# A decoder trunk's last norm in parts: squares a product earlier, scalings in place, and a ring of ten for raw activations

## The chip, the core and the metric

The kernel runs on one core of one Trainium2 chip. The core has five engines with an instruction queue each: TensorE (PE, the matmuls), VectorE (DVE), ScalarE (ACT), GpSimd (POOL) and SyncE (SP, which here only issues transfers). Each queue is worked off in order. The metric is the time of one execution on the device, in microseconds (us), the median over some runs. A profile is one further execution, taken by the hardware profiler.

## The reference

One layer of a decoder in fp32, for 2048 tokens of width 1024, then a last norm. What matters here is the end:

```python
def rmsnorm(x, w):
    xf = x.astype(jnp.float32)
    xf = xf * lax.rsqrt(jnp.mean(xf * xf, axis=-1, keepdims=True) + NORM_EPS)
    return (xf * w.astype(jnp.float32)).astype(x.dtype)

def conv_ffn(h, w_up, conv_w, conv_b, w_down):
    gv = h @ w_up
    g = causal_dwconv(gv[..., :D_FF], conv_w, conv_b)
    v = gv[..., D_FF:]
    return (jax.nn.silu(g) * v) @ w_down
...
        h = rmsnorm(x, ffn_norm_w[i])
        x = x + conv_ffn(h, ffn_w_up[i], ffn_conv_w[i], ffn_conv_b[i], ffn_w_down[i])
    return rmsnorm(x, final_norm_w)
```

D_FF is 2816. The change touches the product with w_down and the last norm.

## The kernel before

**Products in halves.** Every fp32 operand is split in two parts that TensorE takes: `halves` (L95) has ScalarE copy the hi part (L98) and VectorE subtract it for the lo part (L99). `mm3` (L120) adds three matmuls for each block of 128 rows of the contraction: hi by hi (L123), hi by lo (L124), lo by hi (L125), each 128x512. `load` (L109) issues a transfer on SP's queue (L111). `rstd` (L127) makes the root of a norm: a VectorE instruction (L130), then a power on GpSimd (L131).

**Stages.** `trunk` runs its stages one after the other, the last two being `stage_up` (gate and value of the feed-forward block) and `stage_down` (the product with w_down, the residual and the last norm). Both use schemes of seven products of sums of blocks. `stage_up` does them for each of two token blocks and 22 column blocks, in the order 1, 6, 5, 3, 7, 4, 2 (`products`, L1008), with 12 matmuls for each product, so a last group of 84 matmuls stands ahead of `stage_down`. Product number n reads its activations from a pool `Hn` of 8 tiles, and raw weights come into `R` (8 tiles).

**stage_down** has seven products (m = 0 to 6, the table `prods`), each for eight pairs of token tiles (p), that is 56 steps of 33 matmuls (`steps`, L1481). `right(m)` makes the 11 weight blocks of a product: raw tiles of w_down through a ring `R` of four, with a sum of two of them on VectorE (L1447) in the products from m=2 on, then halves into the W rings. The eleven of the next product are made one or two per step of the present one. `left(m, p)` makes the activations of one step, one step ahead: three chunks (4, 4 and 3 blocks, 512, 512 and 384 columns); for each it loads one or two raw tiles into the ring `A` (two, except in m=2 and m=3), adds them in place on VectorE (L1462), and makes halves into the rings C and B of six tiles, three hi and three lo in turn for each step. The result of a step lies in PSUM (a ring of eight) and is added to one or two halves of the 1024-wide accumulators of the tiles, kept in `X` (tiles 0 to 7) and `Y` (8 to 15): the first time by a ScalarE copy (L1504), later by VectorE (L1506). In m=2 and m=3 the residual x2 of a tile is loaded into the ring `O` and added (L1494 to L1497).

**The last norm.** A tile of odd number is complete after its step of m=5, one of even number after its step of m=6. `finish(t)` (L1471) then does all of it: ScalarE squares the tile's 1024 columns into a tile of `O` with the sum beside it (L1474), the root (L130, L131), two scalings of 512 columns into `O` (L1478) and two transfers out (L1479).

**Pools and order.** The names of the pools of a stage are laid out in SBUF in the order of its `k.pools` line, and the next stage's pools use the same memory; a tile that overlaps one of the stage before waits for the last reader of that very tile. `stage_up` has this line:

```python
    wa, ev, up, h1, gp, wb, cp, *hs, rp, sp = k.pools(cx, "u", ("V", 4), ("E", 8), ("U", 4), H(1), ("G", 4, 576), ("W", 14), ("C", 1, 1024), H(3), H(7), H(4), H(2), H(6), H(5),
                                                      ("R", 8), ("S", 2))
```

A pair ("V", 4) is four tiles of 512 columns, a third number another width; H(n) is ("Hn", 8). The order of instructions on each engine is set by the framework's scheduler; it can differ from the order of the code.

Of the kernel before, what the change touches and what calls it, by code (L numbers as in the profile page):

```python
# [9 lines left out]
F32 = mybir.dt.float32  # L10
F32R = mybir.dt.float32r
I32 = mybir.dt.int32
AF = mybir.ActivationFunctionType
ALU = mybir.AluOpType
AX = mybir.AxisListType
P = 128
# [1071 lines left out]
def ring(n, pools):  # L1088

    it = cycle([p for p in pools for _ in range(n)])  # L1090
    return lambda *args: next(it)(*args)
# [327 lines left out]
def stage_down(k, cx, a, d, out, T, NK=11):  # L1419


    nc, tc, V, S, G = k.nc, k.tc, k.V, k.S, k.G
    NT = T // 128

    W = lambda i: (f"W{i}", 8)
    xa, w0, xb, rp, ar, sp, cb, fp, *ws, wr, ca = k.pools(cx, "d", ("X", NT // 2, 1024), W(0), ("Y", NT // 2, 1024), ("O", 2, 1152), ("A", 6), ("S", 2), ("C", 6), ("F", 1, 1024),
                                                          W(3), W(4), W(1), W(2), ("R", 4), ("B", 6))
    wp, ac = ring(8, [w0] + ws[2:] + ws[:2]), ring(6, [ca, cb])

    prods = [(((1, 0), (1, 1), 1), ((0, 0),), ((1, 0, 1), (1, 1, -1))),  # L1430
# [6 lines left out]
    chunks = ((0, 4), (4, 8), (8, 11))  # L1437
    op = lambda s: ALU.add if s > 0 else ALU.subtract

    def right(m):  # L1440
        r = prods[m][1]
        for j in range(NK):
            raws = [k.load(a["w_down"][kh * NK + j][:, dh * 512:dh * 512 + 512], wr()) for kh, dh in r[:2]]
            x = raws[0]
            if len(r) > 1:
                x = sp()
                V.tensor_tensor(x, raws[0], raws[1], op=op(r[2]))  # L1447
            hi, lo = wp(F32R), wp(F32R)
            k.halves(x, hi, lo)
            yield hi, lo  # L1450

    def left(m, p):
        l, got = prods[m][0], []
        for lo_, hi_ in chunks:
            n = (hi_ - lo_) * 128
            raws = []
            for t, kh in l[:2]:
                raw = ar()[:, 0:n]
                k.load(d["act"][2 * p + t][:, kh * NK + lo_:kh * NK + hi_, :], raw.rearrange("p (a n) -> p a n", n=128))
                raws.append(raw)  # L1460
            if len(l) > 1:
                V.tensor_tensor(raws[0], raws[0], raws[1], op=op(l[2]))  # L1462
            h, lw = ac(F32R)[:, 0:n], ac(F32R)[:, 0:n]
            k.halves(raws[0], h, lw)
            got += [(h[:, j * 128:j * 128 + 128], lw[:, j * 128:j * 128 + 128]) for j in range(hi_ - lo_)]
        return got
    acc, here = {}, set()
    fw = fp()
    G.dma_start(out=fw, in_=a["final_norm_w"].partition_broadcast(P))

    def finish(t):  # L1471
        x, xs = acc[t], rp()[:, 0:1024]
        ss = k.sm.tile([P, 1], F32, tag="ss", name="ss")
        S.activation(xs, x, AF.Square, accum_out=ss)  # L1474
        k.rstd(ss, ss, 1.0 / 1024, 1e-6)
        for nh in range(2):
            s = slice(nh * 512, nh * 512 + 512)
            V.scalar_tensor_tensor(xs[:, s], x[:, s], ss[:, 0:1], fw[:, s], op0=ALU.mult, op1=ALU.mult)  # L1478
            nc.sync.dma_start(out=out[t * 128:t * 128 + 128, s], in_=xs[:, s])  # L1479
    NP = NT // 2  # L1480
    steps = [(m, p) for m in range(7) for p in range(NP)]  # L1481
    gen = right(0)
    Lh = {steps[0]: left(*steps[0])}
    W = list(gen)
    for n, (m, p) in enumerate(steps):
        if p == 0:
            Wn, gen = [], right(m + 1) if m < 6 else None
        for t, dh, _ in prods[m][2]:
            t += 2 * p
            if t not in acc:  # L1490
                acc[t] = xa() if t < NT // 2 else xb()
        if n + 1 < len(steps):
            Lh[steps[n + 1]] = left(*steps[n + 1])
        if m in (2, 3):  # L1494
            x, xt = rp()[:, 0:1024], (m - 2) * NP + p
            nc.sync.dma_start(out=x, in_=d["x2"][xt * 128:xt * 128 + 128, :])
            V.tensor_tensor(acc[xt], acc[xt], x, op=ALU.add)  # L1497
        ps = k.ps()
        k.mm3(ps, [(*l, *w) for l, w in zip(Lh.pop((m, p)), W)])
        for t, dh, sign in prods[m][2]:  # L1500
            o = acc[2 * p + t][:, dh * 512:dh * 512 + 512]
            if (2 * p + t, dh) not in here:
                here.add((2 * p + t, dh))
                S.activation(o, ps, AF.Copy, scale=float(sign))  # L1504
            else:
                V.tensor_tensor(o, o, ps, op=op(sign))  # L1506
        if gen:
            for _ in range(2 if p else 1):
                w = next(gen, None)
                if w:  # L1510
                    Wn.append(w)
            if p == NP - 1:
                Wn += list(gen)
        if p == NP - 1:
            W = Wn
        if m >= 5:
            finish(2 * p + (1 if m == 5 else 0))


def trunk(tc, a, out, T):  # L1520
    with ExitStack() as cx:
# [28 lines left out]
        with ExitStack() as c1:  # L1550
            stage_down(k, c1, a, d, out, T)
# [40 lines left out]
```

## Time and profile before

| | us |
|---|---|
| median of three runs | 2668.95 (2668.3 to 2670.01) |
| profiled execution, its own time | 2667.42 |
| its span, first to last instruction | 2665.7 |
| PE busy in the span | 2603.0 |
| DVE, ACT, POOL busy | 2121.5, 1358.0, 407.3 |

The profiled execution lies 1.5 us below the median. PE is by far the busiest engine. In the timelines below, an engine that issues transfers has a q behind its name (SPq), and the time given for an issue group is that of the issues, not of the transfers. "[0.73 <-POOL ss L131]" behind a row says that the engine was idle for 0.73 us before it, and that the instruction of L131 on POOL released it. Rows of equal instructions that follow one another directly are one row with their count (x2).

### The profile page before, as it was taken

How to read it: one execution, taken by the hardware profiler on the slowest of the kernel's cores; microseconds unless marked ns; L12 is line 12 of the kernel's file. 1: busy time of each engine (PE TensorE's matmuls, PEld its weight loads, DVE VectorE, ACT ScalarE, POOL GpSimd, SP SyncE). 2: the span in 40 equal slices, each digit the busy share in tenths (PEclk: the TensorE clock that was granted, in tenths of full speed). 3: DMA queues.
4: the chain of work that ended last, by engine and by line, in shares of the span. 5: the costliest groups of instructions: out<-in, count | busy, mean ns of one | idle time of the engine just before them, and what ended most of it. 6: DMA issues, size and time to landing. Idle time of an engine off the chain costs nothing. (4 is left out here: it accounts for less than half of the span.)

```text
span 2665.7 us, 38967 instructions
## 1 busy us (share of the span) xinstructions
PE 2603.0 (98%) x12796; PEld 2150.3 (81%) x12796; DVE 2121.5 (80%) x4034; ACT 1358.0 (51%) x2817; POOL 407.3 (15%) x691
## 2 busy tenths in 40 slices
PE   8999999999999999999999999999999999999998
PEld 6768878788987888888888888888888887788876
DVE  8798898888876537778788878989787877678776
ACT  4655567764556116788554545445444434433333
POOL 1112212111022101202202332212111110000000
PEclk9999999999999999999999999999999999999999
DMA  5565554543586936546762444344222218887886
GB/s 188 173 186 175 182 192 164 164 139 126 177 303 235 336 126 213 182 168 231 261 202 83 128 146 133 103 123 153 80 87 80 87 64 280 278 283 249 262 263 209
DMA packets 244355, 480.94 MB, mean 180 GB/s; under 512 B 30584, under 2 KB 72824, under 8 KB 244152
## 3 DMA queue, kind: packets, MB, share of 16 engines
q1 hardware_dynamic: 182312, 341.38, 38.3%
q0 software_dynamic: 32976, 118.09, 13.8%
q10 hardware_dynamic: 28864, 18.98, 2.3%
q8 instruction: 101, 1.65, 0.3%
q14 instruction: 102, 0.84, 0.1%
HBM read 363.25 MB, written 114.49 MB: 179 GB/s over the span
## 5 line engine op out<-in xcount | busy, mean ns | idle before, releaser
L124 PE MATMUL ps<-H,W 128*128 128x512 f32 x952 | 370.6, 389 | 0.3 <-DVE H L99 0.3
L123 PE MATMUL ps<-H,W 128*128 128x512 f32 x952 | 370.8, 390 | 0.0
L125 PE MATMUL ps<-H,W 128*128 128x512 f32 x952 | 370.4, 389 | 0.0
L123 PE MATMUL ps<-h,w 128*128 128x512 f32 (+1 forms) x736 | 299.1, 406 | 3.1 <-DVE h L102 2.1
L124 PE MATMUL ps<-h,w 128*128 128x512 f32 (+1 forms) x736 | 286.6, 389 | 0.9 <-DVE h L102 0.9
L125 PE MATMUL ps<-h,w 128*128 128x512 f32 (+1 forms) x736 | 286.3, 389 | 0.7 <-DVE w L99 0.7
L123 PE MATMUL ps<-Q,A 128*128 128x512 f32 x704 | 275.8, 392 | 0.8 <-ACT A L98 0.8
L125 PE MATMUL ps<-Q,A 128*128 128x512 f32 x704 | 274.5, 390 | 0.2 <-DVE A L99 0.2
L124 PE MATMUL ps<-Q,A 128*128 128x512 f32 x704 | 273.9, 389 | 0.0
L98 ACT ACTIVATE W<-S 128x512 fp32r<-128x512 f32 x191 | 119.0, 630 | 292.8 <-DVE S L1346 146.1
L98 ACT ACTIVATE w<-r 128x512 fp32r<-128x512 f32 x224 | 139.4, 627 | 139.5 <-PE ps L124 108.7
L124 PEld LDWEIGHTS ps<-H,W 128*128 128x128 f32 x952 | 178.7, 188 | 38.0 <-DVE H L99 1.1
L125 PEld LDWEIGHTS ps<-H,W 128*128 128x128 f32 x952 | 178.7, 188 | 37.2
L123 PEld LDWEIGHTS ps<-H,W 128*128 128x128 f32 x952 | 178.7, 188 | 37.0 <-ACT H L98 0.3
L99 DVE TENSOR_TENSOR w<-r,w 128x512 fp32r<-128x512 f32 x224 | 153.5, 687 | 33.0 <-ACT w L98 31.4
L125 PEld LDWEIGHTS ps<-h,w 128*128 128x128 f32 x736 | 139.4, 189 | 30.6 <-DVE w L99 1.1
L123 PEld LDWEIGHTS ps<-h,w 128*128 128x128 f32 x736 | 139.6, 190 | 29.7 <-DVE h L102 2.3
L124 PEld LDWEIGHTS ps<-h,w 128*128 128x128 f32 x736 | 139.8, 190 | 27.6 <-DVE h L102 2.5
L125 PEld LDWEIGHTS ps<-Q,A 128*128 128x128 f32 x704 | 132.2, 188 | 29.1 <-DVE A L99 1.4
L123 PEld LDWEIGHTS ps<-Q,A 128*128 128x128 f32 x704 | 132.2, 188 | 27.8 <-ACT A L98 1.0
L124 PEld LDWEIGHTS ps<-Q,A 128*128 128x128 f32 x704 | 132.3, 188 | 26.6
L98 ACT ACTIVATE A<-F 128x512 fp32r<-128x512 f32 (+1 forms) x146 | 89.1, 631 | 126.4 <-PE ps L124 74.1
(474 smaller groups left out, 6187.4 us busy)
## 6 DMA issues: line engine op xcount, KB each, us to landing
A<-actd SPq DMA_DIRECT2D x192, 256.0 KB, 3.6
r<-in_w_in SPq DMA_DIRECT2D x176, 256.0 KB, 2.9
R<-in_w_up SPq DMA_DIRECT2D x176, 256.0 KB, 2.8
R<-in_w_down SPq DMA_DIRECT2D x132, 256.0 KB, 4.3
actd<-U POOLq DMA_DIRECT2D x88, 256.0 KB, 3.1
A<-actd SPq DMA_DIRECT2D x96, 192.0 KB, 3.6
R<-h3Cd SPq DMA_DIRECT2D x56, 256.0 KB, 3.2
L<-acsd POOLq DMA_DIRECT2D x32, 384.0 KB, 4.4
```

What stands on the lines that cost most here:

```text
L98: self.S.activation(hi, src, AF.Copy)
L99: self.V.tensor_tensor(lo, src, hi.bitcast(F32), op=ALU.subtract)
L123: self.TE.matmul(out, lh, rh, start=first and i == 0, stop=False)
L124: self.TE.matmul(out, lh, rl, start=False, stop=False)
L125: self.TE.matmul(out, ll, rh, start=False, stop=last and i == n - 1)
```

## The change

- The ring `O` is removed; the ring `A` gets ten tiles for six.
- `finish` falls into three parts. `square(t, h)` (L1474) squares one half of 512 columns on ScalarE into a PSUM tile (L1476) and leaves its sum in one of two small tables. For even tiles the second half, and for odd tiles the first, is squared in m=4; the other half as soon as it is complete, in m=6 or m=5. `root(t)` (L1478) adds the two sums on VectorE (L1480) and calls `rstd`. `give(t, h)` (L1483) scales a half in place in `X` or `Y` (L1486) and issues its transfer out (L1487).
- A table `later` calls `root` one step after the last square, and `give` two steps after it (the first half of odd tiles eight steps after it).
- x2 is loaded in halves, through the ring `A`, and added in halves (L1507). The accumulation is now L1514 on ScalarE and L1516 on VectorE.

```diff
--- before.py
+++ after.py
@@ -1423,7 +1423,7 @@
     NT = T // 128
 
     W = lambda i: (f"W{i}", 8)
-    xa, w0, xb, rp, ar, sp, cb, fp, *ws, wr, ca = k.pools(cx, "d", ("X", NT // 2, 1024), W(0), ("Y", NT // 2, 1024), ("O", 2, 1152), ("A", 6), ("S", 2), ("C", 6), ("F", 1, 1024),
+    xa, w0, xb, ar, sp, cb, fp, *ws, wr, ca = k.pools(cx, "d", ("X", NT // 2, 1024), W(0), ("Y", NT // 2, 1024), ("A", 10), ("S", 2), ("C", 6), ("F", 1, 1024),
                                                           W(3), W(4), W(1), W(2), ("R", 4), ("B", 6))
     wp, ac = ring(8, [w0] + ws[2:] + ws[:2]), ring(6, [ca, cb])
 
@@ -1468,15 +1468,23 @@
     fw = fp()
     G.dma_start(out=fw, in_=a["final_norm_w"].partition_broadcast(P))
 
-    def finish(t):
-        x, xs = acc[t], rp()[:, 0:1024]
-        ss = k.sm.tile([P, 1], F32, tag="ss", name="ss")
-        S.activation(xs, x, AF.Square, accum_out=ss)
+
+    sums, later, begun = (d["rs"], d["r8"]), {}, {}
+
+    def square(t, h):
+        begun[t] = begun.get(t, -1) + 1
+        S.activation(k.ps(), acc[t][:, h * 512:h * 512 + 512], AF.Square, accum_out=sums[begun[t]][:, t:t + 1])
+
+    def root(t):
+        ss = sums[0][:, t:t + 1]
+        V.tensor_tensor(ss, ss, sums[1][:, t:t + 1], op=ALU.add)
         k.rstd(ss, ss, 1.0 / 1024, 1e-6)
-        for nh in range(2):
-            s = slice(nh * 512, nh * 512 + 512)
-            V.scalar_tensor_tensor(xs[:, s], x[:, s], ss[:, 0:1], fw[:, s], op0=ALU.mult, op1=ALU.mult)
-            nc.sync.dma_start(out=out[t * 128:t * 128 + 128, s], in_=xs[:, s])
+
+    def give(t, h):
+        s = slice(h * 512, h * 512 + 512)
+        x = acc[t][:, s]
+        V.scalar_tensor_tensor(x, x, sums[0][:, t:t + 1], fw[:, s], op0=ALU.mult, op1=ALU.mult)
+        nc.sync.dma_start(out=out[t * 128:t * 128 + 128, s], in_=x)
     NP = NT // 2
     steps = [(m, p) for m in range(7) for p in range(NP)]
     gen = right(0)
@@ -1492,9 +1500,11 @@
         if n + 1 < len(steps):
             Lh[steps[n + 1]] = left(*steps[n + 1])
         if m in (2, 3):
-            x, xt = rp()[:, 0:1024], (m - 2) * NP + p
-            nc.sync.dma_start(out=x, in_=d["x2"][xt * 128:xt * 128 + 128, :])
-            V.tensor_tensor(acc[xt], acc[xt], x, op=ALU.add)
+            xt = (m - 2) * NP + p
+            for h in range(2):
+                s = slice(h * 512, h * 512 + 512)
+                x = k.load(d["x2"][xt * 128:xt * 128 + 128, s], ar())
+                V.tensor_tensor(acc[xt][:, s], acc[xt][:, s], x, op=ALU.add)
         ps = k.ps()
         k.mm3(ps, [(*l, *w) for l, w in zip(Lh.pop((m, p)), W)])
         for t, dh, sign in prods[m][2]:
@@ -1513,8 +1523,24 @@
                 Wn += list(gen)
         if p == NP - 1:
             W = Wn
-        if m >= 5:
-            finish(2 * p + (1 if m == 5 else 0))
+        at = lambda w, f, *args: later.setdefault(min(n + w, len(steps)), []).append((f, args))
+        if m == 4:
+            square(2 * p, 1)
+            square(2 * p + 1, 0)
+        elif m == 5:
+            square(2 * p + 1, 1)
+            at(1, root, 2 * p + 1)
+            at(2, give, 2 * p + 1, 1)
+            at(NP, give, 2 * p + 1, 0)
+        elif m == 6:
+            square(2 * p, 0)
+            at(1, root, 2 * p)
+            at(2, give, 2 * p, 0)
+            at(2, give, 2 * p, 1)
+        for f, args in later.pop(n, []):
+            f(*args)
+    for f, args in sorted(later.pop(len(steps)), key=lambda v: v[0] is not root):
+        f(*args)
 
 
 def trunk(tc, a, out, T):
```

Three places of the instruction order. The first is SP's queue at the hand-over from `stage_up` to `stage_down`: the last two loads of up weights and the first four of w_down, with the semaphores that each waits for. Before:

```order
L111 DMA R<-in_w_up 128x512 [waits DMAHW7_49,DVE_49]
L111 DMA R<-in_w_up 128x512 [waits DMAHW0_49,DVE_49]
L111 DMA R<-in_w_down 128x512 [waits DMAHW1_49,DMAHW0_49,DVE_49]
L111 DMA R<-in_w_down 128x512 [waits DMAHW3_49,DMAHW2_49]
L111 DMA R<-in_w_down 128x512 [waits DMAHW5_49]
L111 DMA R<-in_w_down 128x512 [waits DMAHW4_49]
```

With the change:

```order
L111 DMA R<-in_w_up 128x512 [waits DMAHW7_49,DVE_49]
L111 DMA R<-in_w_up 128x512 [waits DMAHW0_49,DVE_49]
L111 DMA R<-in_w_down 128x512 [waits DMAHW0_49,DMAHW1_49,DVE_49,PE_49]
L111 DMA R<-in_w_down 128x512 [waits DMAHW5_49,DMAHW3_49,DMAHW2_49]
L111 DMA R<-in_w_down 128x512
L111 DMA R<-in_w_down 128x512 [waits DMAHW4_49]
```

The order is the same; the first load of w_down waits for PE as well.

The second is VectorE's queue over one step of m=6, from one accumulation to the next (X is the accumulator, A raw activations, B and C halves, ss or rs and r8 the sums of squares). Before:

```order
L1506 TENSOR_TENSOR X_24026<-X_24026,ps_27099 128x512
L99 TENSOR_TENSOR B_27167<-A_27161,B_27166 128x384
L1462 TENSOR_TENSOR A_27223<-A_27223,A_27225 128x512
L130 TENSOR_SCALAR ss_27135<-ss_27135 128x1
L1462 TENSOR_TENSOR A_27232<-A_27232,A_27234 128x384
L1478 SCALAR_TENSOR_TENSOR O_27134<-X_24026,ss_27135,F_23353 128x512 x2
L99 TENSOR_TENSOR C_27220<-A_27214,C_27219 128x512
L1462 TENSOR_TENSOR A_27285<-A_27285,A_27287 128x512
L99 TENSOR_TENSOR C_27229<-A_27223,C_27228 128x512
L1506 TENSOR_TENSOR X_24100<-X_24100,ps_27170 128x512
```

With the change:

```order
L1516 TENSOR_TENSOR X_24023<-X_24023,ps_27153 128x512
L99 TENSOR_TENSOR B_27221<-A_27215,B_27220 128x384
L1480 TENSOR_TENSOR rs_91<-rs_91,r8_92 128x1
L1462 TENSOR_TENSOR A_27414<-A_27414,A_27416 128x512
L130 TENSOR_SCALAR rs_91<-rs_91 128x1
L1486 SCALAR_TENSOR_TENSOR X_24023<-X_24023,rs_91,F_23350 128x512 x2
L1462 TENSOR_TENSOR A_27423<-A_27423,A_27425 128x512
L99 TENSOR_TENSOR C_27274<-A_27268,C_27273 128x512
L99 TENSOR_TENSOR C_27283<-A_27277,C_27282 128x512
L1462 TENSOR_TENSOR A_27432<-A_27432,A_27434 128x384
L1516 TENSOR_TENSOR X_24097<-X_24097,ps_27224 128x512
```

Root and scalings of a tile stand behind its own accumulation in both. The sums of raw chunks lie further ahead of their halves: before, A_27223 is summed six rows ahead of its halves; with the change, the three sums of a step are for halves behind the rows shown.

The third is SP's queue at the same place. Before:

```order
L111 DMA A_27287<-actd_90 128x512 [waits DMAHW2_49,DVE_49]
L111 DMA A_27294<-actd_90 128x512 [waits DMAHW7_49,DMAHW4_49,DVE_49]
L1479 DMA out<-O_27134 128x512 [waits DMAHW0_49,DVE_49,Activation_49]
L1479 DMA out<-O_27134 128x512 [waits DMAHW1_49,DVE_49]
L111 DMA A_27296<-actd_90 128x512 [waits DVE_49]
L111 DMA A_27303<-actd_90 128x384 [waits DMAHW6_49,DMAHW3_49,DVE_49]
```

With the change:

```order
L111 DMA A_27423<-actd_90 128x512 [waits DMAHW5_49,DMAHW2_49,DVE_49]
L111 DMA A_27425<-actd_90 128x512 [waits DVE_49]
L111 DMA A_27432<-actd_90 128x384 [waits DMAHW7_49,DMAHW4_49,DVE_49]
L1487 DMA out<-X_24023 128x512 [waits DMAHW0_49,DVE_49]
L1487 DMA out<-X_24023 128x512 [waits DMAHW1_49,DVE_49]
L111 DMA A_27434<-actd_90 128x384 [waits DMAHW6_49,DVE_49]
L111 DMA A_27487<-actd_90 128x512 [waits DMAHW3_49,DVE_49]
```

Two output transfers stand between loads of raw activations in both; the load right behind them is now the second raw tile of a step's last chunk, before it was that of a middle chunk.

## Rows read from the trace of the kernel before

**Rows 1.** The page, part 1: busy us (share of the span) x instructions, each engine.
```profile
PE 2603.0 (98%) x12796; PEld 2150.3 (81%) x12796; DVE 2121.5 (80%) x4034; ACT 1358.0 (51%) x2817; POOL 407.3 (15%) x691
```

**Rows 2.** PE's timeline: start us, us, engine, line, operation, shapes, [idle before <- releaser].
```profile
2201.56 0.39 PE L123 MATMUL ps<-H,W 128*128 128x512 f32 x1
...
2215.16 0.39 PE L123 MATMUL ps<-W,B 128*128 128x512 f32 x1
...
2277.86 0.39 PE L123 MATMUL ps<-W,B 128*128 128x512 f32 x1
...
2344.19 0.39 PE L123 MATMUL ps<-W,B 128*128 128x512 f32 x1
...
2523.71 0.39 PE L123 MATMUL ps<-W,B 128*128 128x512 f32 x1
...
2656.21 0.39 PE L125 MATMUL ps<-W,C 128*128 128x512 f32 x1
```

**Rows 3.** Busy us by stretch: PE, PEld, DVE, ACT, POOL; PEclk, DMA share, GB/s.
```profile
2277.30:2342.30 65.00, 61.28 (x260) 49.27 (x259) 42.94 (x70) 27.80 (x53) 0.00 (x0) 0.97 0.84 274
2342.30:2402.30 60.00, 60.00 (x267) 49.67 (x266) 48.42 (x72) 20.77 (x37) 0.00 (x0) 1.00 0.84 285
...
2462.30:2522.30 60.00, 60.00 (x266) 49.71 (x265) 45.19 (x77) 19.09 (x34) 0.00 (x0) 1.00 0.85 273
```

**Rows 4.** PE's waits, 2215 to 2660: total us, times, longest.
```profile
PE ps L125 <- DVE B L99: 7.4, 6, 2.3
```

**Rows 5.** VectorE's waits, 2587 to 2656.4.
```profile
DVE A L1462 <- DMA A<-actd: 12.3, 13, 2.1
```

**Rows 6.** SP's timeline at the hand-over of the two stages.
```profile
2192.20 14.30 SPq L111 DMA_DIRECT2D R<-in_w_down  x9
```

**Rows 7.** PE's timeline within m=1.
```profile
2314.67 0.50 PE L125 MATMUL ps<-W,B 128*128 128x512 f32 x1 [2.26 <-DVE B L99]
...
2316.61 0.63 PE L123 MATMUL ps<-W,B 128*128 128x512 f32 x1
2317.04 0.63 PE L124 MATMUL ps<-W,B 128*128 128x512 f32 x1
```

**Rows 8.** Timeline of VectorE and ScalarE at the end.
```profile
2653.98 0.68 DVE L1506 TENSOR_TENSOR Y<-Y,ps 128x512 f32<-128x512 f32 x1
...
2658.21 0.68 DVE L1506 TENSOR_TENSOR Y<-Y,ps 128x512 f32<-128x512 f32 x1
2659.05 1.06 ACT L1474 ACTIVATE O<-Y 128x1024 f32<-128x1024 f32 x1 [3.08 <-DVE Y L1506]
...
2660.23 0.15 DVE L130 TENSOR_SCALAR ss<-ss 128x1 f32<-128x1 f32 x1 [1.34 <-ACT O L1474]
```

**Rows 9.** VectorE's timeline, m=4's last accumulation and m=6.
```profile
2530.64 1.28 DVE L1506 TENSOR_TENSOR Y<-Y,ps 128x512 f32<-128x512 f32 x2
...
2627.55 0.69 DVE L1462 TENSOR_TENSOR A<-A 128x512 f32<-128x512 f32 x1 [0.89 <-DMA A<-actd]
2629.23 0.56 DVE L1462 TENSOR_TENSOR A<-A 128x384 f32<-128x384 f32 x1 [0.99 <-DMA A<-actd]
...
2630.58 1.41 DVE L1478 SCALAR_TENSOR_TENSOR O<-X,ss,F 128x512 f32<-128x512 f32 x2 [0.73 <-POOL ss L131]
...
2636.96 0.69 DVE L1462 TENSOR_TENSOR A<-A 128x512 f32<-128x512 f32 x1 [2.09 <-DMA A<-actd]
...
2642.55 0.68 DVE L1506 TENSOR_TENSOR Y<-Y,ps 128x512 f32<-128x512 f32 x1
```

**Rows 10.** SP's timeline in m=6.
```profile
2624.41 0.33 SPq L111 DMA_DIRECT2D A<-actd  x1
...
2631.42 0.94 SPq L1479 DMA_DIRECT2D out<-O  x2
2632.70 0.33 SPq L111 DMA_DIRECT2D A<-actd  x1
```

**Rows 11.** DMA issues, 2587 to 2656.4: count, KB each, median us to landing.
```profile
A<-actd SPq DMA_DIRECT2D x15, 192.0 KB, 3.4
```


## The prediction

> **What bounds the kernel now.** The page's first part says that TensorE is busy for 98% of the span [rows 1], so time is won or lost only where it stands still. I listed the first matmul of each product of the last stage on PE's timeline [rows 2], since the change touches that stage alone. A step is 33 matmuls. The three products from m=2 to m=4 took 2523.71 - 2344.19 = 179.52 for 24 steps, 7.48 each, and the table of stretches shows PE busy for 60.00 of 60.00 us there [rows 3]: 7.48 is a step with no hole. By that measure m=0 (2277.86 - 2215.16 = 62.70, for 59.84) lost 2.86, m=1 (66.33) lost 6.49, and m=5 and m=6 (2656.60 - 2523.71 = 132.89, for 119.68; 0.16 of it because the last matmul shows its whole length) lost 13.05. Behind the last matmul come 2665.7 - 2656.6 = 9.1 us of tail. The list of PE's waits says what it stands for: halves of activation chunks, the costliest line being the lo half that VectorE makes [rows 4]. And in the last product VectorE itself waits most for raw activations, 12.3 us in 13 waits [rows 5]. So the loop that counts there is load, sum, halves, and in between, in the same in-order queue, the root and the scalings of a finished tile.
>
> **The change, part by part**, against the profiled execution (2667.42; the median of the runs is 1.5 higher).
>
> *The pools move by half a slot.* "O" (2 x 1152 columns, 4.5 slots of 512) goes and "A" takes 10 slots for 6, so S, C, F, the later W pools, R and B begin half a slot earlier. Before, each of these lay exactly on pools of the stage before. Counted along the two pools lines, the first slot of R (raw w_down) now reaches into the last slot of "H5", which the last product group of the stage before still reads. SP's order shows it: the first w_down load has a new wait on PE. Before, it was issued at 2192.20 [rows 6], and the first product began 2215.16 - 2192.20 = 22.96 us later. That H5 slot is last read by the third matmul of the group's third product. The product starts at 2201.56 [rows 2] (five products of 12 matmuls before 2215.16), so this matmul ends at 2201.56 + 2 x 0.23 + 0.39 = 2202.4. All that SP loads for this stage stands behind this one load (eleven tiles of w_down through a ring of four, then the activations), so I shift the whole chain: 2202.4 + 22.96 = 2225.4, and PE idles 10.2 us from 2215.16. Two corrections. What m=0 loses today comes from the same late chain and would lie within this gap: -2.86. And after a stand of 2.26 us at 2314.67 eight matmuls started 0.43 apart for 0.23, 1.6 us [rows 7], in a stretch whose granted clock is 0.97 [rows 3], that is with moments at 1.2 GHz; I add the same +1.6 after the longer stand. Sum **+8.9**; bounds 7.3 (full clock) and 11.8 (m=0's losses stay). Nothing covers it, as PE has no other product left.
>
> *Ring of ten, m=1.* Ten raws hold 1.67 steps where six held one, so four more loads are under way before a sum must free a buffer. In m=1 PE waits for loads that are a little late. Between 0 and -6.49 I take **-5**.
>
> *m=5 and m=6: squares, roots, scalings.* One half of each tile is now squared a product earlier, into a PSUM tile: in m=4 two squares a step on ScalarE, which is busy 19.09 of 60.00 us there [rows 3]; hidden. Root and scalings are written as one and two steps later, but VectorE's order shows the adding of the sums, the root and both scalings still in the tile's own step, between its accumulation and the next sums. So the chain stays within the step. New is that the second load of the last chunk stands behind both output transfers on SP and waits for the sum just before, and that VectorE needs the sum of these loads before its next accumulation. One turn of this loop, from start to start: sum to issue 0.72 (0.68 and 0.04), landing L, the 384-wide sum 0.47, accumulation to adding 1.59 (2.02 at the kernel's end, less 0.43 because the square is half as wide, estimated as 0.63 for 1.06), adding 0.17, a sum 0.60, root to scalings 0.88 (0.15 and the wait of 0.73), two scalings 1.33 [rows 8, 9]: 5.76 + L. (A next instruction starts 0.08 before the end of the one ahead, as two of 0.68 take 1.28, so each counts for 0.08 less than its length.) For L the rows give 2627.55 - 2624.41 = 3.14 and, right behind two output transfers, 2636.96 - 2632.70 = 4.26 [rows 9, 10]. I take the middle, 3.7, as the new load too stands behind outputs. A turn is then 9.46. Before, thirteen turns took 2642.55 - 2530.64 = 111.91, 8.61 each [rows 9]. 13 x 0.85 = +11.1; against that the longer ring gives two thirds of a step of lead, once: -5.0. Sum **+6**; with L = 3.14 it is -1, with 4.26 +13.3, and -13.05 is the floor.
>
> *x2 in halves, m=2 and m=3.* One load of 512 KB becomes two of 256 KB through the A ring, and one addition two, 16 times. PE has no hole there, VectorE is busy 48.42 of 60 us [rows 3], and these products take 3 raws a step, so 5 of 10: 0. Without that cover the one more instruction of VectorE would cost at most its 0.68 less 0.08.
>
> *Tail.* The last tiles run serially through VectorE: accumulation to accumulation 2658.21 - 2653.98 = 4.23 [rows 8], since root and scalings of one tile stand ahead of the next. Each such chain becomes 0.26 shorter (half square -0.43, adding +0.17). The last accumulation cannot start before 2656.65, 1.56 earlier than now, and its own chain saves 0.26. Between -0.8 (three chains) and -1.8 I take **-1.3**.
>
> *Sum:* 8.9 - 5 + 6 - 1.3 = +8.6: 2676.0 for the profiled execution, **2677.5** on the median's scale.
>
> **Rivals.** (1) *The terms cancel.* If L is as in the shorter row, m=5 and m=6 give -1, and the sum is +1.6: 2670.5. For it: VectorE's 13 waits for loads average under 1 us. Against: the load now stands behind outputs, as the one of 4.26 did. (2) *Faster.* Short landings bring the loop of m=5 and m=6 below today's. It decides at L = 2.63: 13 x (2.63 + 5.76 - 8.61) - 5 = -7.9, with the other terms -5.3. At the floor of all terms the sum is 8.9 - 6.49 - 13.05 - 1.3 = -11.9: 2657. Against it: in the last stretch the median landing of loads of 192 KB is 3.4 [rows 11]. The Trainium skill ("DMA: Bandwidth & Descriptors", section "Anatomy of one DMA") fits a transfer as 2.0 us plus its bytes at 436 GB/s; by that estimate 192 KB land in 2.45 us, m=5 and m=6 give -10.2, and the kernel takes 2661. The trace does not agree: 3.4 for this size, with several transfers under way. (3) *Much slower.* L = 4.26 in each turn: +15.9, 2685; with no gain in m=1 either, 2690. (4) That the change does not do what it says, in that "later" is not later in VectorE's order, is part of the forecast.
>
> **How the numbers follow.** About 0.2%, 5.3 us, is what a measurement of this kernel can tell from no change. The forecast (+5.3 to +12) gets 0.47. Rival 1 gets 0.27. Rival 2 gets 0.10, as its loads would have to land faster than this median. Rival 3 gets 0.16. So faster 0.10, same 0.27, slower 0.63. The range, 2665 to 2688, takes in rival 1 and most of rival 3, and leaves out rival 2 and the worst of rival 3.
>
> **What would show it.** On PE's timeline a gap from 2215 to about 2225, the first w_down load at about 2202 on SP's, a lower granted clock right behind the gap; steps of 7.5 in m=1; in m=6 accumulations 9 to 10 us apart with a wait for a load ahead of the 384-wide sum, and that load issued right behind two outputs; a tail of about 8. I am wrong if the first product starts before 2220, or if steps of m=6 come at 7.5 to 8.

## The result: slower by 0.8%, more than forecast

| | before | with the change |
|---|---|---|
| median of six runs | 2668.72 us (2665.46 to 2673.15) | 2689.35 us (2685.6 to 2694.4) |
| ratio | | 1.0077, 95% interval 1.0063 to 1.0091 |
| span of the profiled execution | 2665.7 | 2683.8 |

The kernel became slower by 20.6 us in the medians and by 18.1 in the profiled executions. The forecast was slower by 8.6 (2677.5), with a range up to 2688.

First the view in which the forecast was made: starts of products on PE's timeline with the change, to be held against [rows 2]. The first row is the last matmul of the stage before.

```profile
2216.55 0.39 PE L125 MATMUL ps<-H,V 128*128 128x512 f32 x1
2226.61 0.79 PE L123 MATMUL ps<-W,B 128*128 128x512 f32 x1 [9.67 <-ACT B L98]
2227.20 0.63 PE L124 MATMUL ps<-W,B 128*128 128x512 f32 x1
2227.62 0.63 PE L125 MATMUL ps<-W,B 128*128 128x512 f32 x1
...
2288.68 0.39 PE L123 MATMUL ps<-W,B 128*128 128x512 f32 x1
...
2348.52 0.39 PE L123 MATMUL ps<-W,B 128*128 128x512 f32 x1
...
2468.78 0.40 PE L123 MATMUL ps<-W,B 128*128 128x512 f32 x1
...
2534.48 0.39 PE L123 MATMUL ps<-W,B 128*128 128x512 f32 x1
...
2676.26 0.39 PE L125 MATMUL ps<-W,C 128*128 128x512 f32 x1
```

A gap of 9.8 us has opened ahead of the first product, and the matmuls behind it start 0.43 apart, in a stretch with a granted clock of 0.96, that is at 1.2 GHz for a while. The page's first line and two stretches (columns as in [rows 3]) are now:

```profile
PE 2606.6 (97%) x12796; PEld 2150.2 (80%) x12796; DVE 2126.0 (79%) x4066; ACT 1358.2 (51%) x2849; POOL 406.5 (15%) x691
```

```profile
2226.60:2288.60 62.00, 61.99 (x264) 51.11 (x265) 45.63 (x77) 30.17 (x56) 0.00 (x0) 0.96 0.94 323
...
2468.70:2534.40 65.70, 62.27 (x266) 48.84 (x265) 51.32 (x86) 28.87 (x67) 0.00 (x0) 1.00 0.81 268
```

Of the 18.1 us more in the span, PE is busy for 3.6 (a matmul behind the gap takes 0.63 for 0.39) and stands for the other 14.5. m=1 (2288.68 to 2348.52, 59.84) has no hole left. m=4 (2468.78 to 2534.48) takes 65.70 where it took 59.84, and m=5 with m=6 take 142.0, up to 2676.5. From such starts I made one table for all kernels of this study: what each product takes beyond 7.48 us a step, the gap ahead of m=0, and the tail from the last matmul's slot to the end of the span. The moment at which the stage before ends differs by some us between executions (2214.93 before, 2216.55 here), so this table, and not the span of one execution, says what an edit does. Each row is one execution, and rows scatter too: before, e2, e6, e7 and e9 have the same order of instructions on VectorE, ScalarE and SP in m=0 and m=1, and yet lose 2.9 to 4.7 in m=0 and 3.4 to 6.8 in m=1. A difference of less than some 3.5 between two rows says nothing by itself.

| kernel | gap | m=0 | m=1 | m=2, 3 | m=4 | m=5, 6 | tail |
|---|---|---|---|---|---|---|---|
| before | 0 | 2.9 | 6.5 | 0 | 0 | 13.1 | 9.3 |
| the change | 9.8 | 2.2 | 0 | 0.6 | 5.9 | 22.3 | 7.3 |
| e1_aligned | 12.6 | 1.8 | 0 | 1.3 | 8.2 | 22.7 | 7.3 |
| e2_norm_only | 0 | 4.2 | 3.4 | 0 | 0 | 22.3 | 8.0 |
| e3_x2_only | 0 | 4.2 | 3.2 | 9.2 | 5.6 | 18.9 | 9.2 |
| e4_x2_own | 15.8 | 2.2 | 3.2 | 2.2 | 0.7 | 23.2 | 7.3 |
| e5_r_aligned | 10.3 | 2.5 | 0 | 4.6 | 6.6 | 23.8 | 7.3 |
| e6_no_later | 0 | 4.4 | 3.5 | 0 | 0 | 17.8 | 8.0 |
| e7_inplace_only | 0 | 4.6 | 4.1 | 0 | 0 | 15.5 | 9.1 |
| e8_after_no_x2 | 9.9 | 2.3 | 0 | 0 | 0 | 20.8 | 7.4 |
| e9_order | 0 | 4.7 | 6.8 | 0 | 0 | 5.7 | 8.0 |
| e10_after_outs_pool | 9.9 | 2.7 | 0 | 1.6 | 5.8 | 28.0 | 9.0 |
| e11_after_order | 9.9 | 2.6 | 0 | 2.5 | 6.1 | 2.9 | 7.3 |
| e12_handover | 8.0 | 2.1 | 0 | 2.1 | 6.0 | 21.5 | 7.3 |

So with the change: gap and m=0 +9.2, m=1 -6.5, m=2 to m=4 +6.4, m=5 and m=6 +9.3, tail -2.0. That is 16.5; the other 1.6 is the later end of the stage before.

### The profile page after: what moved, and what is told of

The parts are those of the page before. It is cut to its first block, busy times and chain, and to the rows that moved or that the text cites. A ratio compares the mean times of both kernels' runs of the same rounds, so it can differ in the third digit from the quotient of the medians.

```text
span 2683.8 us, 38956 instructions
## 1 busy us (share of the span) xinstructions
PE 2606.6 (97%) x12796; PEld 2150.2 (80%) x12796; DVE 2126.0 (79%) x4066; ACT 1358.2 (51%) x2849; POOL 406.5 (15%) x691
## 4 chain that ended last, share of the span: by engine, by line
PE 66%; DVE 6%; DMA 5%; ACT 2%; issue 2%; POOL 0%; SPq 0%; ACTq 0%; DVEq 0%; POOLq 0%
PE ps L125 21%; PE ps L123 20%; PE ps L124 20%; DMA A<-actd 2%; DMA R<-in_w_down 1%; PE ps L148 1%; PE ps L457 1%; DVE A L1462 1%; DMA F<-VWd 1%; PE ps L1068 0%; DMA R<-h3Cd 0%; PE ps L462 0%; PE ps L828 0%; DVE W L99 0%; DMA R<-in_w_up 0%
```

## What the trace shows of the three losses

**The hand-over.** SP's timeline and the list of what SP waits for:

```profile
2204.05 15.17 SPq L111 DMA_DIRECT2D R<-in_w_down  x10
2219.28 2.83 SPq L111 DMA_DIRECT2D A<-actd  x6
```

```profile
SPq L111 <- PE ps L125: 10.2, 1, 10.2
```

The first w_down load waits 10.2 us for PE and is issued at 2204.05, against 2192.20 in [rows 6], as forecast.

**VectorE's lead before m=4.** Its waits for x2, first in the kernel before, then with the change (2225 to 2480: us in total, times, longest):

```profile
DVE Y L1497 <- DMA O<-x2d: 2.3, 3, 1.6
DVE X L1497 <- DMA O<-x2d: 1.1, 1, 1.1
```

```profile
DVE X L1507 <- DMA A<-x2d: 18.9, 7, 5.9
DVE Y L1507 <- DMA A<-x2d: 8.4, 5, 3.0
```

Together that is 27.3 us where it was 3.4. The sum of its waits does not show that x2 is to blame, for others became shorter: those for activations fell from 36.9 to 14.3 us and those for w_down from 16.7 to 10.1, and in all VectorE stood 70.1 us for 66.4. What counts is the lead. While m=2 and m=3 ran, PE lost almost nothing by these waits, because VectorE works ahead: it makes the halves of a step while PE still has one or two steps to go. How far ahead shows at the first lo half that m=4 needs. Before, it was begun at 2452.32 for a step that began at 2463.87:

```profile
2452.32 0.69 DVE L99 TENSOR_TENSOR B<-A,B 128x512 fp32r<-128x512 f32 x1 [0.87 <-ACT B L98]
```

With the change it was begun at 2467.50 for 2468.78:

```profile
2467.50 0.69 DVE L99 TENSOR_TENSOR B<-A,B 128x512 fp32r<-128x512 f32 x1
```

A lead of 11.6 us has become 1.3. In m=4 VectorE is a little slower than PE in both kernels; before, PE lived on the lead for all of m=4 and three steps of m=5; now it stands for 0.6 us in the last step of m=3 and for 2.0 in the third of m=4.

**The loop of m=5 and m=6.** VectorE's timeline around one turn, up to the accumulation of m=5's seventh step (2612.41) and the half behind it, SP's, and PE's next stand:

```profile
2606.66 1.42 DVE L1486 SCALAR_TENSOR_TENSOR Y<-Y,rs,F 128x512 f32<-128x512 f32 x2 [0.66 <-POOL rs L131]
2607.99 0.69 DVE L1462 TENSOR_TENSOR A<-A 128x512 f32<-128x512 f32 x1
2608.59 1.28 DVE L99 TENSOR_TENSOR B<-A,B 128x512 fp32r<-128x512 f32 x2
2611.93 0.56 DVE L1462 TENSOR_TENSOR A<-A 128x384 f32<-128x384 f32 x1 [2.05 <-issue]
2612.41 0.68 DVE L1516 TENSOR_TENSOR Y<-Y,ps 128x512 f32<-128x512 f32 x1
2613.01 0.55 DVE L99 TENSOR_TENSOR B<-A,B 128x384 fp32r<-128x384 f32 x1
```

```profile
2607.44 1.00 SPq L1487 DMA_DIRECT2D out<-Y  x2
2608.70 1.52 SPq L111 DMA_DIRECT2D A<-actd  x3
```

```profile
2618.02 0.50 PE L125 MATMUL ps<-W,C 128*128 128x512 f32 x1 [0.80 <-DVE C L99]
```

This is the loop of the forecast: sum at 2607.99, load at 2608.70 (0.71 later, just behind the end of that sum), 3.23 later the 384-wide sum at 2611.93 behind a stand of 2.05, and only then the accumulation and the last half of the step that PE is in. PE does not wait for this half, but for the first lo half of the next step, which comes behind it in the same queue (begun at 2617.28): 13.2 of PE's 16.1 us of stands in m=5 and m=6 lie ahead of a step's third matmul, the first that needs a lo half. The raw chunk that holds up the queue belongs to a step nearly two steps ahead.

## The experiments

**e1, e5, e12: the hand-over.** e1 aligns all pools with an unused tile, e5 only R and B, e12 all from W3 on, with an order of loads:

```diff
e1, in the pools line of the change:
-("A", 10), ("S", 2)
+("A", 10), ("Q", 1, 256), ("S", 2)
e5:
-W(2), ("R", 4)
+W(2), ("Q", 1, 256), ("R", 4)
e12 (first is the last load of left(0, 0)):
-("F", 1, 1024), W(3)
+("F", 1, 1024), ("Q", 1, 256), W(3)
...
+                if m == 0:
+                    with tc.issue_after(first):
+                        w = next(gen, None)
```

> The changed kernel with a tile of 256 columns, never used, behind the ring of ten, so that every pool from S on lies again on whole tiles of the stage before. Theory (hand-over): the wait of the first w_down load on PE goes, PE's gap of 9.8 us ahead of the first product goes, and the time falls by 8 to 10 us, to about 2680; the losses of m=4 to m=6 (28.8 us) stay. Rival (the gap has another cause, such as the longer ring of activation loads in SP's queue): the gap stays at 8 us or more and the time at about 2689.

> The changed kernel with 256 unused columns right ahead of R alone: R and B lie again on whole tiles of the stage before, the pools S to W2 stay half a tile early, and SP issues ten w_down loads and then six activation loads, as with the change. Theory (the prediction's): the wait of the first w_down load for PE sets the hand-over; the first load is back at about 2192 and the gap ahead of the first product falls from 9.8 us to under 2. Rival: the fifth weight tile (first of W1, which still reaches into the last tile of H2, read by the stage's very last product) holds the chain just as long; the first load is at about 2192 and the gap is still 8 us or more.

> The changed kernel with 256 unused columns behind F, so that W3 to B lie on whole tiles of the stage before, and the w_down loads of the second product kept behind the first step's activations in SP's queue. Theory (the half tile and the order of loads explain the gap): the gap ahead of the first product falls from 9.8 us to 4 or less. Rival (the ring of ten also changes VectorE's order at the hand-over: the first sum stands behind the last convolution of the stage before): the gap is 6 us or more, with the first sum right behind the last instructions of that stage.

Measured: e1 2690.08 us, ratio 1.0082 (1.0067 to 1.0097); e5 2691.32 and e12 2681.26 in one execution each. No gap went. In e5 the first load is back at 2192.57 and the activations still come at 2218.03, the ten loads being spread over 25.4 us:

```profile
2192.57 25.41 SPq L111 DMA_DIRECT2D R<-in_w_down  x10
2218.03 2.34 SPq L111 DMA_DIRECT2D A<-actd  x5
```

In the order of VectorE the fifth and sixth weight block stand behind the last addition of the stage before (their W pool reaches into H2, which PE's last product reads), and the ring of four lets no load past them:

```profile
2215.73 0.69 DVE L1389 TENSOR_TENSOR G<-ps,E 128x512 f32<-128x512 f32 x1 [2.03 <-PE ps L125]
2216.33 1.28 DVE L99 TENSOR_TENSOR W<-R,W 128x512 fp32r<-128x512 f32 x2
```

So e5's rival holds: there are two waits, and the second alone is enough for the gap. Whether the first alone would be was not run. In e1 no pool is shifted, but the scheduler puts 19 w_down loads ahead of the first activation:

```profile
2191.39 27.81 SPq L111 DMA_DIRECT2D R<-in_w_down  x19
2219.25 2.83 SPq L111 DMA_DIRECT2D A<-actd  x6
```

In e12 the loads are in time (the activations at 2210.05), and the first sum stands behind the last convolution instructions of the stage before:

```profile
2216.09 2.78 DVE L1413 SCALAR_TENSOR_TENSOR U<-G,C,U 128x512 f32<-128x512 f32 x4 [0.94 <-POOL G L1406]
2218.91 1.35 DVE L1415 TENSOR_TENSOR U<-U,E 128x512 f32<-128x512 f32 x2
2220.18 0.68 DVE L1462 TENSOR_TENSOR A<-A 128x512 f32<-128x512 f32 x1
```

All kernels with a ring of eight or ten have the gap, those with six have none. No single wait was shown to make the gap: taking one away left another that ended as late, so what the runs tie it to is the change of memory and order as a whole. An arrangement of ten raw tiles without the gap was not found here.

**e2, e3, e4, e8: x2 or the norm.** e2 is the change without the ring and with x2 as before; e3 is the kernel before with x2 alone changed; e4 gives x2 two half tiles of its own, with eight raw tiles; e8 is the change without x2 (the residual is missing in its output).

```diff
e2, against the change:
-("A", 10)
+("O", 2, 1152), ("A", 6)       and x2 whole, from rp(), in one addition
e3, against before:
-            x, xt = rp()[:, 0:1024], (m - 2) * NP + p
+            xt = (m - 2) * NP + p
+            for h in range(2):
+                x = k.load(d["x2"][xt * 128:xt * 128 + 128, s], ar())
e4, against the change:
-("A", 10)
+("O", 2, 640), ("A", 8)        and x2 halves from rp()
```

> Only the norm in parts (early squares, root, scalings in place); ring of six, x2 as before in whole tiles through its own ring, pools as before. Theory A (x2 through the ring of raw activations is what takes VectorE's lead away before m=4): m=2 to m=4 lose nothing, m=5 and m=6 lose about 13, the tail is 1 to 2 shorter, the time 2664 to 2669. Theory B (the norm in parts itself: its squares in m=4, its root chain in m=5 and m=6): m=4 loses about 6 and m=5 with m=6 over 20, the time is 2680 or more.

> The kernel before with x2 alone changed: loaded in halves through the ring of raw activations, which stays at six; the old norm with its own ring stays. Theory A: VectorE waits for x2 in m=2 and m=3 for 15 us or more (3.4 before), its lead at the start of m=4 is under 4 us (11 before), m=4 to m=6 lose 25 to 30 us and the time is 2680 to 2685. Theory B: nothing changes, 2668.

> The changed kernel with a ring of eight for raw activations, a ring of two half tiles for x2 alone (2 x 640 columns), and thereby all pools on whole tiles of the stage before. Theory A: no gap at the hand-over, m=1 loses 2 or less, m=4 nothing, m=5 and m=6 at most 13, tail 1 to 2 shorter: 2658 to 2665. Theory B: m=4 to m=6 lose 25 or more all the same: 2672 to 2678.

> The changed kernel with x2 neither loaded nor added; all else as with the change. Theory A (x2 in the ring of raw activations takes VectorE's lead): the lead at the start of m=4 is 8 us or more (1 with the change), m=4 loses 1 or less (6.4 with the change), the time is 7 to 13 below the changed kernel's. Rival (the early squares or the ring itself slow m=4): m=4 still loses 5 or more.

Measured: e2 2675.04 us, 1.0022 (1.0012 to 1.0032); e3 2685.65, 1.0066 (1.0051 to 1.0081); e4 2692.85, 1.0085 (1.0068 to 1.0102); e8 2680.59 in one execution. Theories A and B both hold in part; the times of e2 and e4 lie outside both forecasts. x2 through the ring of raw tiles is enough by itself: e3 loses 15 us in m=2 to m=4 and 6 more behind. Its waits for x2:

```profile
DVE Y L1499 <- DMA A<-x2d: 16.7, 10, 4.6
DVE X L1499 <- DMA A<-x2d: 16.4, 9, 3.3
```

e8 shows it from the other side: without x2, m=2 to m=4 lose nothing. VectorE's lead before m=4, measured as above, divides the kernels the same way: 11.3 to 11.6 us in the six that do not load x2 through the raw ring or do not load it at all (before, e2, e6, e7, e8, e9), 0.8 to 1.3 in the seven that do, and 6.6 in e4. e4 says that the place is not the point: two half tiles of its own hold one tile of x2 instead of two, VectorE waits 19.1 us for them, and m=3 has holes again. No run gave x2 in halves the room of two whole tiles, so halves and room are not told apart. (e4's gap of 15.8 is another story: there the first raw tiles wait for the convolution weights of the stage before.) And e2 shows the second cause, without any x2: m=5 and m=6 lose 22.3 with the norm in parts alone. e2 also clears the early squares: m=4 loses nothing with them.

**e6, e7, e10: what in the norm.** e6 is e2 without the table: root and both scalings called at once. e7 is the kernel before with scalings and outputs in the accumulator, nothing else. e10 is the change with outputs issued by GpSimd.

```diff
e6, against e2 (and so for the others of m=5 and m=6):
-            at(1, root, 2 * p)
-            at(2, give, 2 * p, 0)
+            root(2 * p)
+            give(2 * p, 0)
e7, against before:
-            V.scalar_tensor_tensor(xs[:, s], x[:, s], ss[:, 0:1], fw[:, s], op0=ALU.mult, op1=ALU.mult)
-            nc.sync.dma_start(out=out[t * 128:t * 128 + 128, s], in_=xs[:, s])
+            V.scalar_tensor_tensor(x[:, s], x[:, s], ss[:, 0:1], fw[:, s], op0=ALU.mult, op1=ALU.mult)
+            nc.sync.dma_start(out=out[t * 128:t * 128 + 128, s], in_=x[:, s])
e10, against the change:
-        nc.sync.dma_start(out=out[t * 128:t * 128 + 128, s], in_=x)
+        G.dma_start(out=out[t * 128:t * 128 + 128, s], in_=x)
```

> The norm in parts alone (ring of six, x2 in whole tiles through its own ring, pools as before), with root and both scalings called at once instead of one and two steps later. Theory C (the table of later calls is what moves the sums of raw chunks behind the scalings): m=5 and m=6 lose about 13 in place of 22, the time is 2662 to 2668. Theory D (the order comes from the shorter norm itself): they lose 18 or more, 2671 or more.

> The kernel before with one edit: the scalings write into the accumulator and the outputs are sent from there; squares are 1024 wide as before, into the ring O, which now waits for no output. VectorE keeps two sums between the accumulation and the scalings. Theory D: m=5 and m=6 lose 13 or less, since no scaling waits for an output and the order is that of before; tail 8 to 9; time 2660 to 2668. Rival (scaling in place is itself slow, by outputs or by its accumulators): m=5 and m=6 lose 18 or more, 2672 or more.

> The changed kernel with the output transfers issued by GpSimd, so that none stands ahead of a load in SP's queue; VectorE's order in m=6 stays that of the change. Theory of the prediction (the load behind two outputs sets the loop): landings ahead of the 384-wide sum get shorter, accumulations come under 8.5 apart, m=5 and m=6 lose 15 or less (22 with the change), time 2680 to 2684. Rival (that load waits for the sum just ahead of it, since the ring is full; the outputs stand there for nothing): the loss stays at 20 or more, 2687 to 2692.

Measured: e6 2671.52 us, 1.0013 (1.0003 to 1.0022); e7 2670.65, 1.0001 (0.9987 to 1.0015); e10 2693.20, 1.0094 (1.0076 to 1.0112). e6 loses 17.8 in m=5 and m=6, just short of theory D's 18 and far from C's 13: by these rows the table is about half of e2's additional 9.2, a share that the scatter leaves uncertain. e7 loses 15.5, between its two bounds, and its time is that of before: scaling in place is neither the gain nor the loss. e10 goes to its rival: without outputs in SP's queue the loss is 28.0 and not smaller. The load waited for the sum ahead of it, as the ring was full; the outputs stood there for nothing. The rows of the loop above show it too: both outputs are issued by 2608.44, the sum ends at 2608.68, and the load follows at 2608.70. Why e10 loses more than the change is not shown.

**e9, e11: the order by hand.** Both fix VectorE's order in m=5 and m=6 with the framework's order-only edges (an instruction is only placed behind another on its engine), from the third step of m=5 on: accumulation, last half, first sum of the next step, root, scalings, first half, second and third sum, second half. Every raw tile is then summed one landing after its buffer came free, and no sum stands between a step's halves that waits for a load. e9 does it to e7 (ring of six), e11 to the change (ring of ten, root and scalings at once). The cut shows the order of the activations; the remarks behind # are added here.

```diff
+        if pin:
+            get(0, seen["lo", s - 1])              # sum 0 behind the last half of the step before
+            x = half(0, seen.get(("fin", s - 3)))  # half 0 behind the last scaling
+            x = get(2, get(1, x))                  # sums 1 and 2 behind half 0
+            half(1, x)
+            x = half(2, seen["V", s - 2])          # half 2 behind the accumulation
```

> The kernel before with scalings in place (as in e7_inplace_only) and VectorE's order in m=5 and m=6 set by hand: accumulation, last half, first sum, root, scalings, first half, second and third sum, second half; every sum then stands at least one landing behind the instruction that freed its buffer. Theory (the order of sums and their landings in VectorE's queue sets the pace of m=5 and m=6): accumulations come 7.5 to 8.2 us apart, m=5 and m=6 lose 6 or less (13 before, 15 with scalings in place alone), time 2658 to 2664. Rival (bandwidth or the number of raw buffers sets the pace, whatever the order): 13 or more lost, 2668 or more.

> The changed kernel (ring of ten, x2 through it, early squares, scalings in place) with root and scalings called at once and VectorE's order in m=5 and m=6 set by hand as in e9_order. Theory (the order, and not the ring, the parts or the outputs, costs the 9 us more in m=5 and m=6): m=5 and m=6 lose 4 to 12 (22 with the change), accumulations in m=6 come under 8 apart, the time is 2675 to 2682; the gap at the hand-over and the losses of m=4 stay. Rival (starting without lead, or the ring, keeps m=5 and m=6 slow): they lose 18 or more, 2686 or more.

Measured: e9 2660.17 us, 0.9963 (0.9951 to 0.9976), faster than both kernels; e11 2665.87, 0.9991 (0.9978 to 1.0004), 23 us below the change's own 2689.35 and below its own forecast of 2675 to 2682. m=5 and m=6 together lose 5.7 in e9 and 2.9 in e11, though e11 enters them with nearly as poor a lead as the change (2.9 us for 1.9). One step of m=6 in e11:

```profile
2619.03 0.68 DVE L1544 TENSOR_TENSOR X<-X,ps 128x512 f32<-128x512 f32 x1
2619.63 0.55 DVE L1480 TENSOR_TENSOR C<-A,C 128x384 fp32r<-128x384 f32 x1
2620.10 0.68 DVE L1474 TENSOR_TENSOR A<-A 128x512 f32<-128x512 f32 x1
2620.70 0.15 DVE L1508 TENSOR_TENSOR rs<-rs,r 128x1 f32<-128x1 f32 x1
2620.89 0.15 DVE L130 TENSOR_SCALAR rs<-rs 128x1 f32<-128x1 f32 x1
2621.70 1.41 DVE L1514 SCALAR_TENSOR_TENSOR X<-X,rs,F 128x512 f32<-128x512 f32 x2 [0.66 <-POOL rs L131]
2623.03 0.69 DVE L1480 TENSOR_TENSOR B<-A,B 128x512 fp32r<-128x512 f32 x1
2623.64 1.16 DVE L1474 TENSOR_TENSOR A<-A 128x512 f32<-128x512 f32 x2
2625.16 0.69 DVE L1480 TENSOR_TENSOR B<-A,B 128x512 fp32r<-128x512 f32 x1 [0.36 <-ACT B L1479]
2625.77 0.68 DVE L1544 TENSOR_TENSOR X<-X,ps 128x512 f32<-128x512 f32 x1
```

The turn is 6.74 us, below PE's 7.48, with the same instructions and no wait for a load. So in m=5 and m=6 it was the order that set the pace: e9 keeps the ring and the transfers of e7, e11 those of the change and its norm in parts (without the table), and most of the loss goes all the same.

## Why the prediction was wrong, step by step

By the parts the change costs 16.5, where the forecast had 8.6. Of the 7.9 between them x2 makes 6.4 and m=5 with m=6 3.3; m=1 and the tail took back 1.5 and 0.7.

**Hand-over, +8.9: right in size, too simple in cause.** Gap and m=0 measured +9.2. The first load came at 2204.05 (2202.4 forecast, with the last group 1.6 later than before), PE started 22.56 us after it (22.96 forecast). The slow matmuls behind the gap are there at 0.43 apart. But that load was not the only holder: e5 took its wait away and kept the gap. A second wait ends about as late (a gap of 10.3 in e5); that it added nothing to the size is luck. The half slot that I named for R holds for the W pools as well, and I left those out.

**m=1, -5: right.** -6.5, all that there was to win: all seven kernels with a ring of ten lose nothing there, e4 with eight 3.2, those with six 3.2 to 6.8.

**x2 in halves, 0: the step that failed.** It read "PE has no hole there" as cover. There was none to see because VectorE ran 11 us ahead; with the change it waited 27.3 us for x2, and the lead that went was missing in the last step of m=3 and in m=4 (together +6.4). The step counted instructions and buffers (5 of 10 in use), and did not ask when the load of x2 can be issued: only when a raw tile comes free, just ahead of its addition in an in-order queue, where before there was room for two whole tiles ahead. On SP's timeline 27 of the 32 halves are issued 0.03 us behind the instruction of VectorE that frees a raw tile; from issue to addition it is 4.4 us in the median, 6.4 before.

**m=5 and m=6, +6: right in mechanism, wrong in the credit for the ring.** Thirteen turns, from the accumulation of m=4's last step to that of m=6's fifth, are these:

```profile
2545.14 1.28 DVE L1516 TENSOR_TENSOR Y<-Y,ps 128x512 f32<-128x512 f32 x2
...
2662.03 0.68 DVE L1516 TENSOR_TENSOR Y<-Y,ps 128x512 f32<-128x512 f32 x1
```

They took 2662.03 - 2545.14 = 116.89, 8.99 each: slower than the 8.61 of [rows 9], but less than the 9.46 forecast. L, from issue to sum, was 3.23 in the turn shown, and 2.55 to 4.25 in the eleven turns that stand before the 384-wide sum, 3.3 on average, where I had 3.7. So the turns cost 13 x 0.38 = 4.9 where I had 11.1. The rest lies mostly ahead of them: the first of these accumulations came 10.7 us after m=5's first matmul, where it had been 6.9, and VectorE's lead there was 1.9 for 6.0. Against that I had credited 5.0 for the longer ring, and this term failed: e2 with a ring of six and the change with ten lose the same 22.3. How much of the 9.3 is the missing lead's stays open. With the norm of before it may cost 5.8 (e3), but e8, with the norm in parts and a lead of 6.4, still loses 20.8, and e2, with 5.3, the whole 22.3. The loop's reason was half right: the load stood behind a full ring, not behind the outputs (e10).

**Tail, -1.3: right.** 9.3 became 7.3; the last accumulation began at 2676.69, right behind the last matmul, as the bound of -1.8 had it; -2.0 lies just beyond that bound.

**The rivals.** Rival 3 (2685, or 2690 with no gain in m=1) is nearest to the time, but not by its mechanism: m=1 gained all there was, and L was about 4.2 in four turns of m=5 alone and 2.6 to 3.2 behind them. What the list lacked was one rival: that a stage without holes gives up its lead.

The Trainium skill ("DMA: Bandwidth & Descriptors", section "Anatomy of one DMA") gives its fit for transfers that GpSimd issues, while the loads here are SP's, which the prediction did not say. By that fit 192 KB take an estimated 2.45 us; the trace with the change does not agree, though it comes nearer: the median from issue to landing was 2.7 in m=6, for 3.4 before [rows 11].

## What to carry to other kernels

A stretch in which the busiest engine never stands may still be where time is lost: read how far the feeding engine runs ahead (the end of an operand's preparation against the start of its use), and price an edit by what it takes of that lead and where the lead would be spent. A larger ring gave m=1 its loss back and gave nothing in m=5 and m=6, where consumers stand further ahead in an in-order queue; in the order by hand, which removed the loss, each of them stands at least one measured landing behind whatever frees its buffer, and ahead of nothing urgent. When pools of a new stage change size, follow every overlap with the stage before, not the first one found.

## What the runs showed that was not expected

The same instructions of VectorE in m=6 took 8.2 to 10.8 us a step (up to the fifth) in the scheduler's order and 6.74 in an order by hand, with the same transfers: 19 us of the kernel lay in the order of some ten instructions. And issuing outputs from GpSimd instead of SP, which took them out of the loads' queue, gained nothing (28.0 for 22.3 lost).
